# Square tiles on the four quarters of the array for the Gram matrices and low-rank projections of a recurrent branch

## The chip, the cores and the metric

The kernel runs on one core of a Trainium2 chip. The metric is the device time of one execution in microseconds. The engines are named as in the profile: PE is TensorE's matmul, PEld its weight loads, DVE is VectorE, ACT ScalarE, POOL GpSimd, SP the queue that issues the DMAs. L12 is line 12 of the kernel's file.

## The reference

One inference step through two layers of a hybrid backbone with 384 tokens (128 of context, 256 latents) of 1024 features. Each layer is a feed-forward half step, a token mixer and a second feed-forward half step. The mixer has three parallel branches: a windowed attention, a neighbourhood attention, and an RWKV-7 recurrence, one scan for each direction. Only the recurrence is touched here. Cut to what matters:

```python
for d, (wlo, alo) in enumerate(((wlo_f, alo_f), (wlo_b, alo_b))):      # two directions
    logw = -jax.nn.softplus(-(lp['decay_w0'][d] + jnp.tanh(wlo) @ lp['decay_up'][d])) - 0.5
    decay = jnp.exp(-jnp.exp(logw))
    a = jax.nn.sigmoid(lp['iclr_a0'][d] + alo @ lp['iclr_up'][d])
    k_d = k * (1.0 + (a - 1.0) * lp['k_a'])
    y_d, s_d = rwkv_scan(r32, decay, k_d, v32, kk, a, s0[:, d], reverse=(d == 1))

def step(S, inp):                                                       # of the scan
    r_t, w_t, k_t, v_t, kk_t, a_t = inp
    sa = jnp.einsum('bhvk,bhk->bhv', S, -kk_t)
    S = S * w_t[:, :, None, :] + sa[..., None] * (kk_t * a_t)[:, :, None, :] + v_t[..., None] * k_t[:, :, None, :]
    return S, jnp.einsum('bhvk,bhk->bhv', S, r_t)
```

`decay_up` and `iclr_up` are the low-rank projections, of rank 64, to 512 features. There are 8 heads of 64 features.

## The kernel before, in words

A layer goes through a feed-forward part, the two attentions, the recurrence, the mixer's output and a second feed-forward part. In the recurrence the eight heads go in four pairs p. A pair passes three stages: `rwkv_prepare` (the factors of the recurrence, with the low-rank projections), `rwkv_chunks` (each chunk of 64 tokens as a linear map of the state, with the Gram matrices) and `rwkv_scan`. In `rwkv_gen` the chunks of pair p are traced step by step among the scan of pair p - 1 and the preparation of pair p + 1.

Both directions d and both heads e of a pair lie on the two halves of the partitions: `half(e)` is the slice of 64 partitions that begins at 64 e. A matmul whose operands lie on 64 partitions uses 64 rows of the array. The operands of the stage are full float32, and each matmul of the source then makes two weight loads and two matmuls in the trace.

- The low-rank projections (L1425, L1426 and L1434, L1435; tile `up`): for each direction one matmul with 64 rows and all 128 columns of the array, over 384 tokens. `pws` and `pas` are two banks of PSUM each, taken from the tag `rw`, which has two banks in all (`rwp`). ACT reads a whole bank afterwards (tiles `th` and `ta`).
- The Gram matrices (L1499 to L1507; tile `pg`): for each direction, two groups, of four and of two chunks. For each chunk and head one matmul with 64 rows and 128 columns, over 128 columns of `arc`. Head e has its own bank `pg[e]`, from the tag `at`, which has three banks (`atp`). DVE then reads each bank once, masks it and writes `gt`.

Two other products of the stage matter for what follows, and are not touched. The tile `pm` is made of matmuls with 64 rows and 64 columns over 128 columns each, which go round the four quarters of the array in the order (0, 0), (1, 1), (0, 1), (1, 0) of row half and column half; it too takes two banks of the tag `at` for four chunks and then for two. The tile `p` (name `p3` in the code) has the same size of matmul on the two quarters of the diagonal.

The order on each engine is made when the kernel is built. A planner takes the instructions by priority, which is their place in the trace, moved ahead by `tc.high_priority(offset)`, and by its own estimate of when each is ready; a bank of PSUM is handed out to a tile as it comes free. An engine then runs its instructions in that fixed order. `tc.issue_after(x)` puts instructions behind x on its engine.

Dense products (the gates and the other branches' projections, `mixer_fill`) are woven into the recurrence: each small product calls `beside`, which adds a cost to a debt, and as long as the debt is over zero, takes the next step of dense products, of two chunks of 128 features with three matmuls each:

```python
    def beside(k, m, n):
        dense[1] += rate[0] * max(n / 600 / (4 if m <= 32 else 2 if m + k <= P else 1), 0.055)
        while dense[1] > 0 and dense[0] is not None:
            with tc.issue_after(rw_last[0].ins):
                b = next(dense[0], None)
            ...
            dense[1] -= b

    def rmm(out, lhs, rhs, **k):
        rw_last[0] = T.matmul(out, lhs, rhs, **k)
        beside(lhs.shape[0], int(np.prod(lhs.shape[1:])), int(np.prod(rhs.shape[1:])))
```

Here k is the number of rows of the array, m the number of columns, n the columns that stream. The functions:

Of the kernel before, what the change touches and what calls it, by code (L numbers as in the profile page):

```python
# [15 lines left out]
P = 128  # L16
# [51 lines left out]
A1 = 14  # L68
C_FIRST = ["tw", "al", "k0", "r0", "v0", "k1", "r1", "v1"]
# [122 lines left out]
# sets of four groups of 256 modulations; the first two are what the first chunks of features need, then the others  # L192
# [3 lines left out]
def _layout(inp):  # L196
    """Rearranges the inputs (permutations and concatenations only)."""
# [36 lines left out]
    # [l][d][h = (p, e)][v][k] -> [l][(e, k)][p][d][v]  # L234
# [8 lines left out]
def _weights(inp, order):  # L243
    """The large weights as 128 x 128 blocks in the order of their use."""
    f = {k: np.asarray(inp[k]) for k in {o[0] for o in order}}
    arows = np.concatenate([_a_q_cols(m) for m in range(4)])
    n = len(order)
    assert n == WS_UNITS * UNIT
    ws = np.empty((WS_UNITS, P, UNIT, P), next(iter(f.values())).dtype)
    for i, (name, l, k, c) in enumerate(order):  # L250
        rows = arows[P * k : P * k + P] if name == "proj_a" else np.arange(P * k, P * k + P)
        cols = _a_q_cols(c[1]) if isinstance(c, tuple) else slice(c, c + P)
        ws[i // UNIT, :, i % UNIT] = f[name][l, rows][:, cols]
    return ws.reshape(WS_SHAPE)
# [12 lines left out]
def _unlayout(r):  # L267
# [7 lines left out]
    st = r["o_st"].reshape(DEPTH, 2, HD, 4, 2, HD)  # l, e, k, p, d, v  # L275
# [4 lines left out]
class Engine:  # L280
    """An engine that knows its last instruction."""
# [14 lines left out]
def trunk(tc, I, O, order, taps=None, stop=None):  # L296
# [5 lines left out]
    def then(*engines):  # L302
        """Behind the last instruction so far of these engines."""
# [37 lines left out]
    class Stream:  # L341
# [16 lines left out]
        def ahead(self):  # L358
            """Out of the steady state: the unit after the next is split as soon as the last is used up."""
# [22 lines left out]
    def mm3(out, chunks, xs, after=()):  # L382
        """out += sum of W_k^T x_k, with both factors as sums of two float32r parts."""
# [7 lines left out]
    def mm3_steps(out, chunks, xs, step=2):  # L391
        """mm3 in steps of a few chunks, with what each costs."""
# [10 lines left out]
    def split(dst_h, dst_l, src, lo_eng):  # L403
        """src (SBUF or PSUM, float32) = dst_h + dst_l."""
# [30 lines left out]
    def ada_beside(pool, n):  # L435
        """The next n steps with the products on the vector engine: where that has time, and the tensor engine has not."""
# [38 lines left out]
    def ada_flush():  # L475
        """To columns: out[feature, (block, group, stream)]."""
# [20 lines left out]
    ax = [act.tile([P, NTOK], F32, name=f"ax{c}") for c in range(KD)]  # L497
    # (four more columns: see Norm)
# [8 lines left out]
    class Norm:  # L507
        """Layer norm over the features of y = alpha x + gate * out, chunk by chunk as out comes.
        The next phase's input is h = rs g1 (y - mu) + b1, g1 and b1 per feature and stream, rs and mu per token. Its
        first products W^T h run on z = g1 y, before rs and mu are known: rs W^T z - rs mu W^T g1 + W^T b1, with g1 and  # L510
        b1 as four more columns of z."""
# [34 lines left out]
        def add(self, c, po):  # L546
# [4 lines left out]
            if c == 0:  # L551
                # the table of Sqrt is there when it is needed
# [27 lines left out]
        def pilot(self):  # L580
            # about the mean of the first four chunks
# [14 lines left out]
        def products(self, chunks, xs, c):  # L596
            """The products of chunk c of out."""
# [14 lines left out]
        def finish(self, head=iter(())):  # L612
            """head: products of the next phase, in steps, from those on z to the last before h is needed."""
# [47 lines left out]
        def h(self, pool, c):  # L661
            """The next phase's input, in two parts."""
# [11 lines left out]
        def x(self):  # L674
            """alpha times the norm's output."""
# [5 lines left out]
    class Head:  # L681
        """The first products of a phase, on z: two groups of them, each chunk by chunk."""
# [25 lines left out]
        def begin(self, pool, norm, job, at):  # L708
            """The start of the phase: h follows the second group's products chunk by chunk; the first group's results."""
# [37 lines left out]
        def scaled(self, key, out, scale=1.0):  # L747
            """out = rs W^T z - rs mu W^T g1; returns scale W^T b1, a column per stream."""
# [21 lines left out]
    def gated(i, l, name, pool, xs, head, after):  # L770
        """128 features of silu(a) g, in two parts."""
# [70 lines left out]
    axd = es.enter_context(tc.tile_pool(name="axd", bufs=1, space=bass.MemoryType.DRAM))  # L842

    def mixer(l, nxt, next_head, head):
        spill = axd.tile([P, KD, NTOK], F32, name=f"axd{l}")
        gcd = axd.tile([P, KD, NTOK], F32, name=f"gcd{l}")
        with ExitStack() as st:
# [9 lines left out]
            with tc.tile_pool(name=f"rw{l}", bufs=1) as pool:  # L857
# [3 lines left out]
                def add(cost, until=None):  # L861
                    """Queues dense work behind the scans' last instruction."""
# [31 lines left out]
    def gate(l, i, m, th, head=None):  # L894
        """tanh(z / 2): the sigmoid is (1 + tanh(z / 2)) / 2."""
# [12 lines left out]
    def project(l, name, m, th, os):  # L908
        """2 merged += 2 gate * (o @ proj); the gate of branch A is in place."""
# [11 lines left out]
    def front_fill(l, keep, pool, w, oa, need, head):  # L921
        """The dense products beside the attention: what its next pair needs, then others."""
# [21 lines left out]
    def mixer_fill(l, keep, pool, w, ob, gcd):  # L944
        """Projections without a place in a chain: they keep the tensor engine busy beside the scans."""
# [12 lines left out]
    def softmax(pool, views, nk, sinks):  # L958
        """views: score tiles [P, nk] in PSUM; sinks: [P, n or 1] or None."""
# [22 lines left out]
    def transposed(pe, nk, pts):  # L982
        """pts: P^T destinations [P, nk // P, P]."""
# [6 lines left out]
    def token_major(pool, src, tag):  # L990
        """[128 features, 384 tokens] -> [token, block, feature]."""
# [10 lines left out]
    def key_stack(pool, src, e, bufs):  # L1002
        """Keys of one head, src[64 e :, :384], as [hi; hi] and [lo; lo] over the 128 partitions."""
# [9 lines left out]
    def query_stack(pool, src, e):  # L1013
        """Latent queries of one head, src[64 e :, :256], as [hi; lo] (in either order)."""
# [6 lines left out]
    def heads_pair(pool, q_ctx, q_lat, k_ctx, kst, vt, v_cache, bias, sinks, keep, name, done, backward=False):  # L1021
        """Two heads (on partitions 0..63 and 64..127) of both streams -> o^T split in two parts."""
        # context queries: full attention over the context
# [9 lines left out]
        # latent queries: latent keys, then the cached context keys  # L1033
# [44 lines left out]
    def rope(pool, src, dst):  # L1078
        """Rotates the latent columns of src [128, 384] into dst [128, 256]."""
# [9 lines left out]
    def attention(l, pool, keep, w, oa, ob, head, spill):  # L1089
        """Branches A and B, pair of heads by pair of heads, among steps of the dense products."""  # L1090
# [37 lines left out]
        for m in range(9):  # L1128
# [3 lines left out]
            # two pairs at a time: the first part of one before the end of the other  # L1132
# [31 lines left out]
    def branch_a(l, pool, ready, soon, head):  # L1164
        """Windowed grouped-query attention; pair m has the query heads m and m + 4."""
# [39 lines left out]
    def branch_b(l, pool, ready, soon):  # L1205
        """Neighbourhood attention; latent queries in reverse order: the bias is then a forward walk through na_rpb."""
# [45 lines left out]
    C_INDEX = {n: i for i, n in enumerate(["tw", "al", "gl"] + [f"{x}{i}" for x in "krv" for i in range(4)])}  # L1252

    def conv_gen(l, keep, pool, w, names):
        """Projections of the scans' inputs with the short convolution over time."""
        wsh = vcol(l, "w_shift")
        late = []
        for nm in names:
# [17 lines left out]
            elif nm[0] == "k":  # L1276
                # 1 / max(|k k_k|, 1e-12) per token and head
# [25 lines left out]
    def head_sums(out, sq):  # L1303
        """out[token, (block, head)] = sums of sq [128 features of two heads, 384] over each head."""
# [3 lines left out]
    def head_spread(pool, rn):  # L1308
        """[token, (block, head)] -> the same for each feature of the head, [128 features, 384], in PSUM."""
# [15 lines left out]
    def beside(k, m, n):  # L1325
        """Dense work beside a product: the tensor engine slows down where it has too little."""
# [464 lines left out]
```

## Time and profile before

| what | before |
|---|---|
| median of 3 runs | 2443.14 us (2442.91 to 2443.93) |
| span of the profiled execution | 2439.6 us |
| PE busy | 2297.4 us, 94% |
| DVE, ACT, POOL busy | 1696.6, 1056.4, 550.0 us |
| mean granted clock of TensorE | 0.983 of 2.4 GHz |

The span is the time from the first to the last instruction of the profiled execution. The profile gives no other time for that execution: what lies around its span is seen only as the 3.5 us between the span and the median of the timed runs. Busy time of PE is the union of the matmuls' spans, and matmuls overlap one another, so a busy PE does not always stream at its peak. The recurrence lies at 577 to 860 us in the first layer and at 1781 to 2065 us in the second.

### The profile page before, as it was taken

Reading aid. Unit: us, or ns where it says so; the run is one execution under the profiler, and the core shown is the slowest. Engines: PE = TensorE matmul, PEld = TensorE weight load, DVE = VectorE, ACT = ScalarE, POOL = GpSimd, SP = SyncE. Lnnn points to the kernel's source line nnn. Section 1 sums busy time; section 2 is a strip of 40 time slices with the busy share of each in tenths; the row PEclk is TensorE's granted clock in tenths of the full one; section 3 lists DMA queues with packets and bytes.
Section 4 is the critical chain, followed back from the end, with each engine's and each line's share of the span. In section 5 each row is a group of like instructions: output and inputs, shape, how many; then the busy total and the mean of one; then the engine's idle time right before and its main releaser. Section 6 shows DMA issues by size and latency. Waiting matters only on the chain.

```text
span 2439.6 us, 42863 instructions
## 1 busy us (share of the span) xinstructions
PE 2297.4 (94%) x17066; PEld 2106.5 (86%) x17066; DVE 1696.6 (70%) x2865; ACT 1056.4 (43%) x1942; POOL 550.0 (23%) x522
## 2 busy tenths in 40 slices
PE   7999999998899998999999999899989999999998
PEld 5999988897777788999889999889877777889997
DVE  3797886777767568786978954776787674665534
ACT  3333245655545445333243332555555454443332
POOL 2111422101122044211432113310022220542113
PEclk9999999999999999999999999999999999999999
DMA  8575644242111262665546743523321113534332
GB/s 314 193 240 198 191 122 130 84 111 78 40 57 47 72 209 95 191 217 180 180 147 205 244 130 122 154 81 91 112 70 39 51 50 90 204 102 140 130 121 87
DMA packets 125079, 324.54 MB, mean 133 GB/s; under 512 B 31568, under 2 KB 50256, under 8 KB 124880
## 3 DMA queue, kind: packets, MB, share of 16 engines
q1 hardware_dynamic: 124880, 321.81, 41.1%
q8 instruction: 134, 2.20, 0.4%
q14 instruction: 65, 0.53, 0.1%
HBM read 312.06 MB, written 9.70 MB: 132 GB/s over the span
## 4 chain that ended last, share of the span: by engine, by line
PE 71%; DVE 15%; ACT 5%; issue 4%; DMA 3%; POOL 2%; SPq 0%; POOLq 0%; ACTq 0%; DVEq 0%
PE po L399 5%; PE po L398 5%; PE po L397 5%; PE pa L387 4%; PE pg L389 4%; PE pa L388 4%; PE pg L387 4%; PE pg L388 4%; PE pa L389 4%; DVE lo L290 3%; DVE acc L290 2%; PE pz L397 2%; DMA adaw<-wada 2%; ACT hi L290 2%; PE pz L398 2%
## 5 line engine op out<-in xcount | busy, mean ns | idle before, releaser
L290 DVE TENSOR_TENSOR lo<-raw,hi 128x1024 fp32r<-128x1024 f32 (+1 forms) x472 | 583.8, 1246 | 305.9 <-ACT hi L290 303.8
L290 ACT ACTIVATE hi<-raw 128x1024 fp32r<-128x1024 f32 x418 | 441.7, 1058 | 785.0 <-issue 267.5
L290 DVE SCALAR_TENSOR_TENSOR acc<-adaw,cs,acc 128x1024 f32<-128x1024 f32 x224 | 292.3, 1327 | 0.0
L290 POOL TENSOR_TENSOR ul<-si,uh 128x384 fp32r<-128x384 f32 x88 | 126.3, 1435 | 579.3 <-ACT uh L290 579.3
L399 PE MATMUL po<-uh,lo 128*128 128x384 f32 x704 | 238.6, 339 | 6.3 <-DVE lo L290 6.3
L397 PE MATMUL po<-uh,hi 128*128 128x384 f32 x704 | 239.7, 340 | 0.0
L398 PE MATMUL po<-ul,hi 128*128 128x384 f32 x704 | 238.0, 338 | 0.0
L387 PE MATMUL pg<-zh,hi 128*128 128x384 f32 x656 | 224.1, 342 | 9.1 <-DVE si L290 9.1
L388 PE MATMUL pg<-zl,hi 128*128 128x384 f32 x656 | 223.8, 341 | 0.0
L389 PE MATMUL pg<-zh,lo 128*128 128x384 f32 x656 | 223.2, 340 | 0.0
L387 PE MATMUL pa<-zh,hi 128*128 128x384 f32 x632 | 216.2, 342 | 4.9 <-ACT si L290 4.4
L389 PE MATMUL pa<-zh,lo 128*128 128x384 f32 x632 | 213.8, 338 | 0.6 <-DVE lo L290 0.6
L388 PE MATMUL pa<-zl,hi 128*128 128x384 f32 x632 | 214.2, 339 | 0.0
L399 PEld LDWEIGHTS po<-uh,lo 128*128 128x128 f32 x704 | 133.5, 190 | 7.3 <-DVE lo L290 7.3
L397 PE MATMUL pz<-zh,hi 128*128 128x384 f32 x352 | 128.1, 364 | 8.5 <-ACT hi L290 5.7
L397 PEld LDWEIGHTS po<-uh,hi 128*128 128x128 f32 x704 | 133.7, 190 | 2.2 <-issue 0.8
L398 PEld LDWEIGHTS po<-ul,hi 128*128 128x128 f32 x704 | 133.5, 190 | 1.4 <-issue 0.8
L387 PEld LDWEIGHTS pg<-zh,hi 128*128 128x128 f32 x656 | 125.0, 191 | 10.0 <-ACT hi L290 6.7
L399 PE MATMUL pz<-zh,lo 128*128 128x384 f32 x352 | 126.3, 359 | 4.1 <-DVE lo L290 4.0
L387 PEld LDWEIGHTS pa<-zh,hi 128*128 128x128 f32 x632 | 119.1, 188 | 9.8 <-ACT si L290 5.3
L389 PEld LDWEIGHTS pg<-zh,lo 128*128 128x128 f32 x656 | 125.6, 191 | 1.6 <-issue 1.6
L388 PEld LDWEIGHTS pg<-zl,hi 128*128 128x128 f32 x656 | 125.0, 191 | 1.6 <-issue 1.6
(390 smaller groups left out, 5157.4 us busy)
## 6 DMA issues: line engine op xcount, KB each, us to landing
raw<-ws SPq DMA_DIRECT2D x418, 512.0 KB, 3.5
adaw<-wada SPq DMA_DIRECT2D x144, 512.0 KB, 4.8
bm<-rpb SPq DMA_DIRECT2D x64, 64.0 KB, 7.1
axd<-ax SPq DMA_DIRECT2D x16, 192.0 KB, 5.2
gcd<-gt SPq DMA_DIRECT2D x16, 192.0 KB, 4.7
gc<-gcd SPq DMA_DIRECT2D x16, 192.0 KB, 3.4
ax<-axd SPq DMA_DIRECT2D x16, 192.0 KB, 4.8
xt<-xt SPq DMA_DIRECT2D x8, 192.0 KB, 8.6
```

Of the source, the lines that this page charges most:

```text
L290: self.last = f(*a, **k)
L387: T.matmul(out, wh, xh, start=(k == 0), stop=False)
L388: T.matmul(out, wh, xl, start=False, stop=False)
L389: T.matmul(out, wl, xh, start=False, stop=(k == n - 1))
L397: T.matmul(out, wh, xh, start=(k == 0), stop=False)
L398: T.matmul(out, wh, xl, start=False, stop=False)
L399: T.matmul(out, wl, xh, start=False, stop=(k == n - 1))
```

## The change

A matmul of a Gram matrix or of a low-rank projection, with 64 rows and 128 columns of the array, becomes two with 64 rows and 64 columns, one for each half of the columns; all four of a chunk (Gram matrices) or of a pair of directions (projections) are issued in the order of `QUARTERS`. The banks, their readers and all other products stay as they are. Comments are left out of the diff.

```diff
+QUARTERS = ((0, 0), (1, 1), (0, 1), (1, 0))
...
     def rwkv_prepare(l, p, w, pool, x):
...
         pws = [rwp("up") for _ in range(2)]
-        for d in range(2):
-            rmm(pws[d][:, :NTOK], wl[half(d), 0, :], w["tw"][half(d), :], start=True, stop=True)
+        for d, m in QUARTERS:
+            rmm(pws[d][half(m), :NTOK], wl[half(d), 0, half(m)], w["tw"][half(d), :], start=True, stop=True)
...
         pas = [rwp("up") for _ in range(2)]
-        for d in range(2):
-            rmm(pas[d][:, :NTOK], wl[half(d), 1, :], w["al"][half(d), :], start=True, stop=True)
+        for d, m in QUARTERS:
+            rmm(pas[d][half(m), :NTOK], wl[half(d), 1, half(m)], w["al"][half(d), :], start=True, stop=True)
...
     def rwkv_chunks(l, p, w, pool, fix, x):
...
             for c0, n in ((0, 4), (4, 2)):
                 pg = [atp("pg"), atp("pg")]
                 for c in range(n):
-                    for e in range(2):
-                        rmm(pg[e][:, c * P : (c + 1) * P], bk[half(e), c0 + c].rearrange("p d t -> p (d t)"), arc[half(e), :, c0 + c, d, :], start=True, stop=True)
+                    for e, m in QUARTERS:
+                        rmm(pg[e][half(m), c * P : (c + 1) * P], bk[half(e), c0 + c, m, :], arc[half(e), :, c0 + c, d, :], start=True, stop=True)
```

## Rows read from the trace of the kernel before

**Rows 1.** The page: busy time of the engines; the chain that ended last, by engine.
```profile
PE 2297.4 (94%) x17066; PEld 2106.5 (86%) x17066; DVE 1696.6 (70%) x2865; ACT 1056.4 (43%) x1942; POOL 550.0 (23%) x522
...
PE 71%; DVE 15%; ACT 5%; issue 4%; DMA 3%; POOL 2%; SPq 0%; POOLq 0%; ACTq 0%; DVEq 0%
```
**Rows 2.** Windows of both recurrences: length, busy of PE, PEld, DVE, ACT, POOL, clock, DMA.
```profile
577.00:860.00 283.00, 260.94 (x3401) 214.85 (x3400) 199.88 (x416) 140.24 (x265) 59.94 (x87) 0.98 0.18 56
1781.00:2065.00 284.00, 262.70 (x3425) 216.06 (x3424) 201.98 (x423) 140.77 (x266) 60.48 (x87) 0.98 0.19 58
```
**Rows 3.** PE's groups by line, first recurrence: count, busy us, mean ns, idle before.
```profile
L1336 PE MATMUL pg<-arc,bk 64*128 64x128 f32 x192 | 20.3, 293 | 2.1 <-DVE gt L290 1.9
L1336 PE MATMUL p<-atq,xt 64*64 64x128 f32 x192 | 13.7, 273 | 0.0
L1336 PE MATMUL pm<-gt,atq 64*64 64x128 f32 x192 | 12.4, 282 | 1.5 <-DVE rp L290 1.1 <-ACT uv L290 0.4
...
L1336 PE MATMUL up<-al,wl 64*128 64x384 f32 x16 | 7.3, 535 | 0.0
L1336 PE MATMUL up<-tw,wl 64*128 64x384 f32 x16 | 7.3, 535 | 0.7 <-ACT th L290 0.7
```
**Rows 4.** Waits of DVE, first recurrence: who for whom, us in total, times, longest.
```profile
DVE mt L290 <- PE pm L1336: 15.5, 5, 8.2
DVE gt L290 <- PE pg L1336: 15.2, 10, 5.1
```
**Rows 5.** PE's timeline, Gram matrices: start, length, count, idle before.
```profile
595.10 1.60 PE L1336 MATMUL pg<-arc,bk 64*128 64x128 f32 x16
597.04 1.16 PE L1336 MATMUL pg<-arc,bk 64*128 64x128 f32 x8 [0.34 <-DVE gt L290]
...
725.92 1.38 PE L1336 MATMUL pg<-arc,bk 64*128 64x128 f32 x16
727.59 0.93 PE L1336 MATMUL pg<-arc,bk 64*128 64x128 f32 x8 [0.29 <-DVE gt L290]
```
**Rows 6.** Instructions of single tiles: count, shortest, median and longest ns.
```profile
L1336 PE MATMUL pg<-arc,bk x384: 271/272/374, 595.1 to 1995.0; 64*128 64x128 f32 x192
...
L1336 PE MATMUL pm<-gt,atq x384: 268/269/322, 639.9 to 2050.5; 64*64 64x128 f32 x192
...
L1336 PE MATMUL up<-tw,wl x32: 482/535/587, 577.6 to 1947.6; 64*128 64x384 f32 x32
```
**Rows 7.** PE's timeline, products already in quarters or on the diagonal.
```profile
639.92 0.93 PE L1336 MATMUL pm<-gt,atq 64*64 64x128 f32 x16
641.26 1.14 PE L1336 MATMUL pm<-gt,atq 64*64 64x128 f32 x24 [0.40 <-ACT uv L290]
...
643.84 0.65 PE L1336 MATMUL pm<-gt,atq 64*64 64x128 f32 x8 [0.61 <-DVE rp L290]
...
718.27 1.31 PE L1336 MATMUL pm<-gt,atq 64*64 64x128 f32 x30
719.84 0.87 PE L1336 MATMUL pm<-gt,atq 64*64 64x128 f32 x16 [0.27 <-DVE rp L290]
...
772.80 3.11 PE L1336 MATMUL p<-atq,xt 64*64 64x128 f32 x48
```
**Rows 8.** PE's timeline, the low-rank projections of two pairs.
```profile
669.46 0.91 PE L1336 MATMUL up<-tw,wl 64*128 64x384 f32 x2
...
673.10 0.91 PE L1336 MATMUL up<-tw,wl 64*128 64x384 f32 x2
...
743.07 0.91 PE L1336 MATMUL up<-tw,wl 64*128 64x384 f32 x2
743.91 0.44 PE L399 MATMUL pp<-o3h,lo 128*128 128x384 f32 x1
744.28 0.91 PE L1336 MATMUL up<-tw,wl 64*128 64x384 f32 x2
```
**Rows 9.** DVE's timeline, behind two batches of Gram matrices.
```profile
727.11 0.42 DVE L290 TENSOR_TENSOR gt<-pg,con 128x256 f32<-128x256 f32 x1 [3.98 <-PE pg L1336]
728.33 1.62 DVE L290 TENSOR_TENSOR gt<-pg,con 128x256 f32<-128x256 f32 x3 [0.80 <-PE pg L1336]
```
**Rows 10.** Windows around a stretch at half clock; columns as in rows 2.
```profile
755.00:757.00 2.00, 1.22 (x14) 0.79 (x14) 2.00 (x4) 1.35 (x4) 0.53 (x2) 1.00 0.03 8
757.30:760.60 3.30, 3.30 (x11) 3.30 (x12) 1.96 (x3) 0.54 (x2) 1.28 (x1) 0.51 0.39 109
```

## The prediction

> **What bounds the kernel now.** I read the page first: PE is busy 94% of the span, and the chain of work that ended last lies on PE for 71% of it [rows 1]. So a microsecond taken from PE's own stream counts, unless PE then waits for another engine. The change touches the recurrence only, so the windows of its two stretches came next [rows 2]: PE is busy in 523.6 of their 567 us (92%), DVE in 401.9. PE is the tightest engine here as well, with some 43 us in which it waits. The groups by line say what is at stake [rows 3]: in one layer the Gram matrices (`pg`) hold PE for 20.3 us in 192 instructions, the projections (`up`) for 14.6 us in 32. For both layers that is 70 us, or 2.9% of the kernel, and no gain can be larger. The waits show on which side the Gram matrices bind: DVE stands still for them 15.2 us in the first recurrence [rows 4], while PE waits for DVE's masking only 1.9 us [rows 3]. A shorter Gram batch would be felt at once.
>
> **How fast the halves run.** The timeline of the batches [rows 5] and the single durations [rows 6] belong together. A matmul over 384 columns takes 482 ns at the least, one over 128 columns 272 ns, so 256 columns more cost 210 ns, and 128 columns stream for 0.105 us. The batch of eight at 597.04 takes 1.16 us; without the 0.27 us of a single one that is 0.111 us each: one after another. The batch of sixteen at 725.92 takes 1.38 us, or 0.069 us each: partly two at a time. So the two row halves of the array already overlap in part. They can't do so always, since the two heads' banks come free at different times, and a batch of eight behind a wait for DVE is mostly one head.
>
> **The change: Gram matrices.** 192 instructions in a layer become 384, over the same 128 columns. What a round over four quarters costs is in the trace: `pm` has the same shape, the same order of quarters and the same banks [rows 7]. I price it three ways, each for 384 instructions of one layer against 20.3 us.
> - Fast end: from the batch of 8 (0.65 us) to the batch of 30 (1.31 us) each further matmul costs 0.03 us. If a direction's batches are 32 and 16, they take 1.37 + 0.89 = 2.26 us, and eight directions 18.1 us: 2.2 us less.
> - Middle: the five batches shown take 4.90 us for 94 matmuls, 0.052 us each, so 20.0 us: 0.3 us less.
> - Slow end: all of `pm` takes 12.4 us for 192 [rows 3], since some of it is chopped in pairs by dense work, so 24.8 us: 4.5 us more.
>
> The Gram batches are longer than those of `pm`, and none of those shown is chopped, so I take the point halfway between the fast end and the middle: 1.25 us less in a layer, 2.5 us in both, with ends of 4.4 us less and 9.0 us more. The gain isn't half of the 40.6 us, because the halves overlap already, and four quarters at 0.035 us each are three at a time, not four.
>
> **The change: projections.** Of 32 in the kernel, each takes 0.91 us as two instructions [rows 8]. The two of a pair stand apart: 3.64 us at 669, 1.21 us at 743. Both need a bank of the tag `rw`, which has two, and other tiles take them too. A quarter streams the same 384 columns; only its weight load is shorter. A matmul that starts cold shows it: 374 against 272 ns for a half, 322 against 269 ns for a quarter [rows 6], so about 0.05 us less. The planner can put (0, 1) in front of (1, 1), whose bank isn't free. I take it that the two quarters of a direction stay together and run at once: 32 x 0.05 = 1.6 us less. The ends: all four of a pair together hide one projection, about 0.86 us, in 16 pairs, 13.7 us less; all quarters apart add as much for each of 32, 27 us more. Neither is near the rows, since the bank keeps the directions apart and nothing keeps the two quarters of one bank apart.
>
> **What doesn't change.** The debt of dense work is the same: a half adds n / 600, a quarter half of that, twice. Banks, masks and DMAs stay; no DMA is issued or moved. There are 448 more matmuls with as many weight loads, in PE's queue alone; the rates taken from `pm` hold the issue of each, so I add nothing for it. If the offsets of priority, counted in instructions, now reach less far, a weight split may move behind its matmul; I have no row for that, and it is in the width.
>
> **The sum.** 2.5 + 1.6 = 4.1 us off PE. Of PE's time in the recurrence 92% is work and the rest waits, so I let 92% of it reach the end: 3.8 us. The profiled span of 2439.6 us becomes 2435.8 us, and with the 3.5 us between that span and the median, about 2439.3 us: 0.16% less. A change within 0.2% (4.9 us) can hardly be told from none here.
>
> **A page against the trace.** Behind the batches of 16 and 8, DVE masks for 0.42 and 1.62 us [rows 9], about 2.0 us in a direction, against 2.31 us of PE. The masking runs behind each batch, so a shorter batch moves it forward, and it is not yet the longer side. The Trainium skill's "TensorEngine Tiling (Array Packing)", section PSUM Bottleneck, says that packing speeds up the matmuls and not the emptying of PSUM. By it the gain of the Gram matrices would be nothing once the masks set the pace, and the sum would be 1.6 us.
>
> **Rivals.**
> - The quarters pay in full. First form: the Gram matrices reach the fast end, and PE loses 4.4 + 1.6 = 6.0 us, of which 5.5 us arrive: 2437.6 us. Second form: the projections of a pair go four at a time, too, 2.5 + 13.7 us, of which 14.9 us arrive: 2428 us. For it: `pm` holds 0.035 us a matmul over a batch of 30. Against the second form: the directions stand apart in all the rows shown.
> - Four quarters really run at once. A Gram matmul then costs 0.105 / 4 = 0.026 us, 384 of them 10.0 us, and both layers lose 20.6 us; with the 1.6 us, 20.4 us arrive: 2423 us. Against it: `pm` never comes below 0.035 us. The Trainium skill's same page, section Theoretical Speedup, states this case: up to twice for each side of a tile that is 64 or less.
> - The other side: the order of the quarters binds two banks. The output of direction 0 is whole only after (0, 1), which is traced behind (1, 1). If the planner doesn't put it ahead, PE stands at (1, 1) until the second bank is free, and ACT's `th` or `ta`, the dense work and the rest of PE's queue stand behind it. The price is at most the time that lies between the two projections now, 3.64 and 1.21 us, on the mean 2.4 us, in 16 pairs 39 us. It decides from 22% of that (8.7 us, the gain and 0.2%); at 30% the time is 2451 us. For it: the traced order. Against it: the planner fills waits with whatever is ready, as the dense work between the projections shows.
> - The quarters run only two at a time, as `p` does on the diagonal: 13.7 us for 192 [rows 3], so 27.4 us for 384, 7.1 us more in a layer, in both 14.2 us less the 1.6 us: 2455 us. `pm` speaks against it.
> - Nothing is gained: the masks, at 2.0 us in a direction nearly as long as PE's batches, or other waits behind them take it up. 2443 us, give or take 2.
> - The clock isn't one of them, but widens all: behind a stretch in which PE worked 1.22 of 2 us, the granted clock was 0.51 for 3.3 us, 1.2 GHz [rows 10]. One such stretch more or less is 1.7 us.
>
> **How the numbers follow.** The forecast 0.38 (all within 0.2%); the quarters in full 0.18 and 0.12, four at once 0.03 (faster); the banks 0.13 and two at a time 0.05 (slower); nothing gained 0.11 (same). Faster is 0.33, same 0.49, slower 0.18. The likeliest one's own range is 2436 to 2442 us: the sum with one stretch of slow clock either way and the two projections' terms in or out. The range for all reaches down to the second form of the gain, half of which lies below 2428 us (0.06, and 0.03 for four at once), and up to the banks at 30%, half of which lies above 2451 us (0.06), with two at a time (0.05) outside: 0.20 is left out.
>
> **What would show it.** In the profile after: `pg` with 768 instructions, 64 x 64, busy about 19 us in a layer, with batches of 32 of some 1.4 us; `up` with 128 instructions, in fours of about 0.86 us, and the two directions still apart. A batch of `pg` broken by dense work, or `up` in twos with other work between, would make the Gram or the projection term wrong, and PE's wait in front of `up` for ACT or DVE the order of the banks. If PE's busy time falls by 4 us and the span doesn't, the wait that grew names the step.

## The result and the profile after

The changed kernel takes 2479.59 us (median of 4 runs, 2474.05 to 2480.65) beside 2443.53 us before (4 runs): a ratio of 1.0153, interval [1.0133, 1.0172], some 36 us slower. The prediction was 2439.3 us in a range of 2428 to 2451.

The totals of the engines and of the chain (the page, sections 1 and 4) answer to [rows 1]:

```profile
PE 2330.7 (94%) x17514; PEld 2128.2 (86%) x17514; DVE 1696.0 (68%) x2865; ACT 1062.2 (43%) x1946; POOL 550.5 (22%) x522
...
PE 71%; DVE 15%; ACT 5%; issue 4%; DMA 2%; POOL 2%; SPq 0%; POOLq 0%; ACTq 0%; DVEq 0%
```

The windows of the two recurrences, from the first projection of a layer to the last product of its scan, first before, then after (columns as in [rows 2]):

```profile
577.60:861.20 283.60, 261.54 (x3408) 215.40 (x3409) 200.17 (x420) 139.64 (x264) 59.94 (x87) 0.98 0.18 57
1781.80:2063.10 281.30, 260.00 (x3410) 213.74 (x3409) 200.75 (x420) 139.76 (x264) 60.48 (x87) 0.98 0.19 58
```

```profile
581.70:880.90 299.20, 273.28 (x3632) 221.20 (x3633) 199.76 (x420) 142.62 (x266) 61.27 (x87) 0.94 0.18 54
1803.70:2103.00 299.30, 274.93 (x3634) 222.76 (x3633) 199.93 (x420) 142.46 (x266) 61.42 (x87) 0.94 0.17 54
```

Together they are 33.6 us longer: PE is busy 26.7 us longer and waits 6.9 us longer, so its share is as before (91 to 92%). What differs most is the last number but two, the granted clock: 0.94 instead of 0.98. The whole span and its mean clock say how much that is:

```profile
core 0: 2478.9 us, clock 0.969
```

A mean of 0.969 between full and half clock (2.4 and 1.2 GHz) means that 2 x 0.031 of the span, 154 us, ran at half clock; before, at 0.983 of 2439.6 us, 83 us did. Work that fills a microsecond at half clock would have taken half of it, so the 71 us more account for up to 35 of the 39 us between the two spans. (The clock has three digits, so such a difference is good to about 2 us.) That is an upper figure for this pair of executions. Of the 71 us, 17 lie ahead of the first projection, where both kernels issue the same instructions in the same order, so they are chance; 48 lie in the two recurrences, which is 24 of their 33.6 us. Over all four runs of the change (mean clock 0.9705) and 59 runs of before (0.9812) the account gives 27 of 38 us. So the clock has some seven tenths of the loss.

The products show it, and something else as well. These are PE's groups by line in the first recurrence, as in [rows 3]:

```profile
L1338 PE MATMUL pg<-arc,bk 64*64 64x128 f32 x384 | 21.2, 292 | 2.9 <-DVE gt L292 2.5
L1338 PE MATMUL pm<-gt,atq 64*64 64x128 f32 x192 | 14.7, 283 | 0.6 <-DVE rp L292 0.5
L1338 PE MATMUL p<-atq,xt 64*64 64x128 f32 x192 | 14.6, 303 | 0.0
L1338 PE MATMUL up<-tw,wl 64*64 64x384 f32 x32 | 9.2, 529 | 0.9 <-ACT th L292 0.7 <-DVE nkk L292 0.2
L1338 PE MATMUL up<-al,wl 64*64 64x384 f32 x32 | 7.0, 504 | 0.0
```

`pm` and `p`, which the change doesn't touch, take 14.7 and 14.6 us instead of 12.4 and 13.7. For `p` it is the clock: one of them takes 303 ns on the mean instead of 273. For `pm` it isn't: one takes 283 ns beside 282 before, and none of them runs at half clock; its 192 products stand in 24 pieces between other work instead of 16, so fewer of them overlap. So the new order costs PE something besides the clock.

The costliest place for the clock is in the first pair of heads of each layer. Windows there, before and after; the last line of each is the stretch at half clock in the second layer:

```profile
621.00:624.20 3.20, 1.44 (x99) 1.39 (x99) 3.20 (x7) 2.56 (x6) 0.00 (x0) 1.00 0.44 147
624.20:631.00 6.80, 6.25 (x117) 5.45 (x117) 3.10 (x8) 3.13 (x4) 0.00 (x0) 0.50 0.04 13
631.00:640.00 9.00, 9.00 (x161) 6.87 (x162) 4.39 (x9) 6.56 (x14) 0.31 (x2) 1.00 0.19 60
...
1829.10:1835.90 6.80, 6.56 (x143) 6.03 (x145) 2.51 (x8) 3.13 (x4) 0.00 (x0) 0.50 0.01 2
```

```profile
625.90:629.30 3.40, 1.86 (x101) 1.52 (x101) 3.21 (x6) 2.20 (x6) 0.00 (x0) 1.00 0.53 159
629.30:649.80 20.50, 18.55 (x259) 16.07 (x261) 6.35 (x17) 6.06 (x11) 0.00 (x0) 0.50 0.07 27
649.80:655.00 5.20, 5.20 (x62) 3.03 (x61) 0.76 (x4) 5.12 (x12) 0.00 (x0) 1.00 0.01 3
...
1851.30:1871.80 20.50, 19.41 (x266) 16.85 (x265) 6.55 (x17) 6.79 (x13) 0.00 (x0) 0.50 0.08 28
```

In both the clock falls behind a stretch in which PE, waiting for DVE, worked about half the time. Before, it was back after 6.8 us; after, it stayed at 0.50 for 20.5 us, with PE busy 18.55 of them. In both layers that is 27 of the 71 us. The timelines show what PE did, first in the stretch of before, then in the changed kernel's:

```profile
622.76 0.98 PE L1336 MATMUL pz<-yr,gt 16*32 16x16 f32 x96 [2.44 <-DVE yr L290]
...
627.97 0.67 PE L397 MATMUL pc<-zh,hi 128*128 128x384 f32 x1
...
630.31 0.67 PE L397 MATMUL pc<-zh,hi 128*128 128x384 f32 x1
```

```profile
627.30 0.98 PE L1338 MATMUL pz<-yr,gt 16*32 16x16 f32 x96 [3.35 <-DVE k L292]
...
631.98 0.94 PE L1338 MATMUL pz<-xt,gt 32*32 32x16 f32 x54 [1.85 <-issue]
...
639.07 0.67 PE L401 MATMUL pc<-zh,lo 128*128 128x384 f32 x1
...
641.13 0.52 PE L401 MATMUL pc<-zh,lo 128*128 128x384 f32 x1
...
643.86 1.54 PE L1338 MATMUL up<-tw,wl 64*64 64x384 f32 x2
645.20 5.28 PE L1338 MATMUL p<-atq,xt 64*64 64x128 f32 x48
```

In both, PE waits for DVE in front of the first small products (2.44 and 3.35 us), and dense work follows later. One of the new quarters stands in the changed kernel's stretch (two instructions), and it comes late, at 643.86. The rest is the triangular solve (`pz`), dense work (`pc`) and `p`, the same products as before, in another place of the stream. For the planner, the program that orders the instructions of each engine, had put much of the other work elsewhere from the first `up` on: of before's 5329 instructions of DVE, ACT and POOL together, 348 can't be matched in order with the changed kernel's. Up to there the order is the same on every engine. (ACT also loads its tables 44 times instead of 40, 1.28 us each. That isn't the loss: gram_quarters and halves_front60 below, with 40 and 36 loads, are 20 and 24 us slower than before.)

### The profile page after: what moved, and what is told of

The parts are those of the page before. It is cut to its first block, busy times and chain, and to the rows that moved or that the text cites. A ratio compares the mean times of both kernels' runs of the same rounds, so it can differ in the third digit from the quotient of the medians.

```text
span 2478.9 us, 43763 instructions
## 1 busy us (share of the span) xinstructions
PE 2330.7 (94%) x17514; PEld 2128.2 (86%) x17514; DVE 1696.0 (68%) x2865; ACT 1062.2 (43%) x1946; POOL 550.5 (22%) x522
## 4 chain that ended last, share of the span: by engine, by line
PE 71%; DVE 15%; ACT 5%; issue 4%; DMA 2%; POOL 2%; SPq 0%; POOLq 0%; ACTq 0%; DVEq 0%
PE po L401 5%; PE po L400 5%; PE po L399 5%; PE pa L389 4%; PE pg L391 4%; PE pg L389 4%; PE pg L390 4%; PE pa L390 4%; PE pa L391 4%; DVE lo L292 3%; PE pz L399 2%; ACT hi L292 2%; PE pz L401 2%; PE pz L400 2%; DVE acc L292 2%
```

## The experiments

Two theories. **A:** the quarter tiles themselves keep the granted clock low. **B:** the new order of all other work does. The table holds every kernel run; "span" and "clock" are of the profiled execution. "Clock's part" is (1 - clock) x span less the 41.5 us that this gives for before; "rest" is what of the difference in span it leaves. Both come from one execution of a kernel, and executions of one kernel differ: the profiled one of halves_front60 is 8 us slower than its three others. By the mean clock over all runs of a kernel, as above for the change, the clock's part is 28 of 44 us for quarters_priority_held, 18 of 29 for halves_front60, 30 of 33 for halves_in_after_order and 9 of 10 for quarters_in_old_order.

| kernel | us | ratio to before | span less 2439.6 | clock | clock's part | rest |
|---|---|---|---|---|---|---|
| the change | 2479.6 | 1.0153 [1.0133, 1.0172] | +39.3 | 0.969 | 35.3 | 4.0 |
| gram_quarters | 2458.1 | 1.0083 [1.0063, 1.0103] | +15.4 | 0.975 | 19.9 | -4.5 |
| proj_quarters | 2460.1 | 1.0091 [1.0068, 1.0114] | +16.3 | 0.976 | 17.4 | -1.1 |
| quarters_by_direction | 2476.6 | 1.0146 [1.0116, 1.0177] | +33.5 | 0.970 | 32.7 | 0.8 |
| quarters_priority_held | 2484.1 | 1.0184 [1.0156, 1.0212] | +43.9 | 0.970 | 33.0 | 10.9 |
| halves_front60 | 2467.2 | 1.0103 [1.0085, 1.0122] | +34.2 | 0.970 | 32.7 | 1.5 |
| halves_back220 | 2447.6 | 1.0027 [1.0012, 1.0042] | +11.1 | 0.976 | 17.3 | -6.2 |
| quarters_warm | 2490.7 | 1.0201 [1.0158, 1.0243] | +61.9 | 0.970 | 33.5 | 28.4 |
| halves_warm | 2477.7 | 1.0157 [1.0129, 1.0184] | +37.6 | 0.978 | 13.0 | 24.6 |
| gram_back120 | 2462.5 | 1.0090 [1.0068, 1.0111] | +17.6 | 0.975 | 19.9 | -2.3 |
| gram_front55 | 2455.6 | 1.0051 [1.0036, 1.0067] | +15.8 | 0.973 | 24.8 | -9.0 |
| gram_fill | 2481.9 | 1.0162 [1.0140, 1.0183] | +45.6 | 0.973 | 25.6 | 20.0 |
| quarters_fill | 2490.9 | 1.0196 [1.0181, 1.0211] | +49.4 | 0.963 | 50.6 | -1.2 |
| quarters_in_old_order | 2450.2 | 1.0046 [1.0030, 1.0062] | +15.6 | 0.975 | 19.9 | -4.3 |
| gram_in_old_order | 2444.6 | 1.0014 [0.9998, 1.0031] | -1.7 | 0.982 | 2.4 | -4.1 |
| proj_in_old_order | 2456.1 | 1.0055 [1.0034, 1.0075] | +18.5 | 0.974 | 22.4 | -3.9 |
| quarters_rows | 2464.8 | 1.0105 [1.0081, 1.0129] | +25.7 | 0.971 | 30.0 | -4.3 |
| halves_in_new_order | 2457.4 | 1.0068 [1.0042, 1.0094] | +17.1 | 0.973 | 24.8 | -7.7 |
| halves_in_after_order | 2471.3 | 1.0132 [1.0107, 1.0157] | +27.1 | 0.971 | 30.0 | -2.9 |

**One part alone (gram_quarters, proj_quarters).** One edit is undone, here the projections' (shown for one of its two places; the other kernel undoes the Gram matrices'):

```diff
-        for d, m in QUARTERS:
-            rmm(pws[d][half(m), :NTOK], wl[half(d), 0, half(m)], w["tw"][half(d), :], start=True, stop=True)
+        for d in range(2):
+            rmm(pws[d][:, :NTOK], wl[half(d), 0, :], w["tw"][half(d), :], start=True, stop=True)
```

> Only the Gram matrices in quarters, the projections in halves as before. Theory A (the quarters themselves keep the granted clock low: time goes with their number, 768 of 896 are here): 2470 to 2478 us. Theory B (the planner's changed order of the other work leaves a sparse stretch, and the clock falls there; what is in quarters does not matter): any value from 2435 to 2480 us, with the half-clock time of the profile explaining the difference to 2443.5 within 6 us (half of the extra time at half clock). The recorded rival of the two banks speaks of the projections alone: 2441 us.

> Only the projections in quarters, the Gram matrices in halves as before. Theory A: 2446 to 2450 us, since only 128 of 896 quarters are left. Theory B: any value from 2435 to 2480 us, again with the difference equal to half of the extra time at half clock within 6 us. The recorded rival of the two banks: nearly the whole loss is here, 2470 to 2480 us, with a wait of PE in front of `up`.

Each costs some 20 us, whether it brings 768 instructions in quarters or 128. Theory A, by the number of quarters, missed both: 2458 instead of 2470 to 2478, and 2460 instead of 2446 to 2450. The clock accounts for both differences within 5 us.

**Another order of the quarters (quarters_by_direction), and the planner's counter held (quarters_priority_held).**

```diff
-QUARTERS = ((0, 0), (1, 1), (0, 1), (1, 0))
+QUARTERS = ((0, 0), (0, 1), (1, 0), (1, 1))
```

```diff
-    def rmm(out, lhs, rhs, **k):
+    def rmm(out, lhs, rhs, back=0, **k):
         rw_last[0] = T.matmul(out, lhs, rhs, **k)
+        tc.cur_priority -= back
...
```

In the second, each call of the change passes `back=m`, 0 for the first half of the columns and 1 for the second.

> All in quarters, but traced in the order (0, 0), (0, 1), (1, 0), (1, 1), so that the two quarters of one bank stand together. The planned order of the other engines is nearly that of the changed kernel (12 of 2867 vector instructions moved). The recorded rival of the two banks: the loss goes, 2435 to 2448 us. Theories A and B: it stays, 2470 to 2485 us.

> All in quarters, but the second quarter of each half does not advance the counter of priorities, so that the planner's offsets reach as far as with halves; the planned order differs from both kernels. The products are those of the changed kernel. Theory A: 2474 to 2484 us. Theory B: the time moves with the order, by 10 us or more from 2479.6, and again the difference to 2443.5 equals half of the extra time at half clock within 6 us.

The first answers the recorded rival of the two banks: with the quarters of a bank together the loss stays, 2476.6 us, so that rival falls. (In the changed kernel's first recurrence PE waits 0.9 us in front of `up`, and 0.7 before.) The second moved the order, but not the time by the 10 us that theory B asked for, and 10.9 us of it is not the clock: a miss for that account. Its time is what theory A expected, to 0.1 us, so this run by itself speaks for A.

**Halves in another order (halves_front60, halves_back220).** No quarter is in these kernels; an offset of the planner is another.

```diff
-OA = 50
+OA = 60
```

```diff
-OB = 200
+OB = 220
```

> The kernel before, all in halves; only the planner's offset for the front work of the next pair is 60 instead of 50, which moves 344 of 2867 vector instructions to other places, more than the quarters do. The products are those of before. Theory A (quarters keep the clock low): no loss, 2434 to 2444 us. Theory B (a moved order does it, halves or quarters): slower, 2445 to 2480 us, with the difference equal to half of the extra time at half clock within 6 us.

> The kernel before, all in halves, with the planner's offset for the chunk work 220 instead of 200 (186 of 2867 vector instructions moved). Theory A: 2434 to 2444 us. Theory B: between 2440 and 2480 us, by the same account of the half-clock time; one of the two reordered kernels at least is over 10 us slower.

Both are slower. The first loses two thirds of what the quarters do, 24 us by the medians, at a clock of 0.970 in the profiled run and 0.975 to 0.976 in the others. Theory A can't say why.

**Products that fill the wait (quarters_warm, halves_warm).** Into the bank of the first small products, ahead of the transpose that they wait for, go two products that nothing reads (WARM is 2), and likewise one ahead of each of the next two transposes:

```diff
+                pz1 = atp("pz1")
+                for _ in range(WARM):
+                    T.matmul(pz1, C("ident"), ty.rearrange("p a b -> p (a b)"), start=True, stop=True)
                 V.transpose(yr.rearrange("p u (b c) -> p c b u", c=16), ty)
```

> The changed kernel with products added that nothing reads: two of 128 x 128 over 512 columns into the bank of the first small products, and two into that of the second, where TensorE waits for the vector engine's transposes. Theory A: the quarters still keep the clock low, 2474 to 2490 us. Theory B: the long stretch at half clock of the first pair (20.5 us in each layer) shrinks to 7 us or less, which gives back some 7 us in each layer; the added products cost at most 1 us a pair; 2460 to 2475 us.

> The kernel before with the same added products. Both theories: its stretches at half clock in the recurrence are short (6.8 and 3.4 us), so little is to be had, 2434 to 2446 us. With the kernel of quarters it shows whether the added products take away what the quarters seem to cost: theory B has the two within 15 us of each other, theory A 35 us or more apart.

In the kernel of quarters, windows of the first pair:

```profile
619.00:622.60 3.60, 0.16 (x1) 0.16 (x2) 3.30 (x6) 1.58 (x3) 0.00 (x0) 1.00 0.23 92
622.60:626.00 3.40, 3.40 (x5) 1.32 (x6) 2.96 (x6) 0.58 (x2) 0.00 (x0) 0.50 0.46 159
626.00:640.00 14.00, 14.00 (x366) 10.85 (x365) 6.24 (x15) 7.01 (x14) 0.00 (x0) 1.00 0.11 29
```

With full-width products in that place the clock is back after 3.4 us (6.8 in the second layer), not 20.5, though the quarters are all there. But the time rose: the added products keep PE busy some 20 us a layer, not 4 (in the groups of the first recurrence, 11.1 and 8.5 us), and other stretches at half clock came up later, 17.1 us from 704.5 and 20.5 us from 1936.7 on. The place is confirmed, the price of 2460 to 2475 us missed. The halves with the same products, expected at 2434 to 2446 us, took 2477.7 us: the price was missed there too. The two kernels are 13 us apart, as theory B asked (within 15) and theory A didn't (35 or more).

**Nearer orders and more dense work (gram_back120, gram_front55, gram_fill, quarters_fill).** `OC = 120` instead of 100, `OA = 55` instead of 50, and for the last two:

```diff
-RATES = (0.4, 0.2, 0.8, 0.3)
+RATES = (0.4, 0.4, 0.8, 0.3)
```

> Gram matrices in quarters, projections in halves, and the planner's offset for the scan of the pair before 120 instead of 100. That brings the order of the vector, scalar and GpSimd instructions nearer to that of before: 236 moved, against 376 with 100. The quarters are the same 768. Theory A (the quarters keep the clock low): no change from 2458, 2453 to 2465 us. Theory B (the order): the loss shrinks with the distance; the halves with 244 moved lost 6.6 us (a ratio of 1.0027) and the Gram quarters by themselves seem to give 4 us, so 2436 to 2450 us.

> Gram matrices in quarters, projections in halves, the planner's offset for the front work 55 instead of 50 (280 instructions moved against before, between the 236 and the 376 of the others). Theory A: 2453 to 2465 us. Theory B: 2438 to 2455 us, with the half-clock account within 6 us.

> Gram matrices in quarters, projections in halves, and twice as much dense work woven in beside the products of the second stage of a chunk (rate 0.4 instead of 0.2), just ahead of the small products in which the clock fell. Theory A: 2453 to 2465 us. Theory B: the long stretch at half clock of the first pair (20.5 us) is shorter, 2440 to 2455 us; if the dense work is then missing later, a stretch appears elsewhere and the time stays.

> The changed kernel, all in quarters, with the same doubled rate of dense work in the second stage of a chunk. Theory A: 2474 to 2484 us. Theory B: 2450 to 2472 us where the long stretches at half clock shrink; unchanged if they only move. Half-clock account within 6 us in either case.

Here theory B was too simple. Both nearer orders came out inside theory A's range and above theory B's. The count of moved instructions doesn't predict the time: 236 gave 2462 us, 280 gave 2456, 376 gave 2458. More dense work made both kernels slower; with all in quarters, the clock's part rose from 35 to 51 us, while with the Gram matrices alone 20 of the 45.6 us are not the clock's. Theory B's account by the clock, within 6 us, fails in seven of the table's nineteen lines, so an order can cost in other ways too.

**The two by two table (quarters_in_old_order, gram_in_old_order, quarters_rows, halves_in_new_order).** A list gives each instruction the place that it had in another kernel's plan as its priority, so that tiles and order can be changed separately. Only quarters_rows has no list: its plan is the planner's own, and the halves get it. In all kernels of quarters here and in the next pair the two quarters of a bank stand together, as in quarters_by_direction, and are charged for dense work as one half. The list:

```diff
+            self.tc.cur_priority = 10 * int(PLAN[Engine.count % len(PLAN)])
+            Engine.count += 1
             self.last = f(*a, **k)
...
```

> All in quarters, but every instruction gets as its priority the place that it has in the plan of the kernel before (the quarters that of their half), so that the order of all engines is that of before: 36 of some 6000 instructions off TensorE moved. Theory A (the quarters keep the granted clock low, in any order): 2465 to 2482 us, half-clock time 130 us or more. Theory B (the moved order does it): the time of before or a little less, 2436 to 2446 us, half-clock time 70 to 95 us.

> Gram matrices in quarters, projections in halves, in the order of the kernel before (4 instructions off TensorE moved). Theory A: 2455 to 2462 us, as with its own order. Theory B: 2434 to 2443 us: the order of before, less the 2 to 5 us by which the Gram matrices are shorter in quarters.

> All in quarters in the planner's own order, the two quarters of a half together and charged for dense work as one half. Its order differs from before in 778 places. It is the partner of the halves in its order. Theories A and B: slower than before, 2455 to 2495 us.

> All in halves, but with the places of the plan of that kernel of quarters as priorities: 128 instructions off TensorE moved against it, 370 against before. Theory A: no quarters, so the time of before, 2436 to 2446 us. Theory B: the order costs the halves as it costs the quarters, 2452 to 2495 us, and within 12 us of the kernel of quarters in that order.

Neither theory is right alone. In the old order the quarters lose 0.46%, 11 us, not 36, and not nothing; halves in an order of the quarters lose 0.68%, 17 us; the quarters in that order lose 1.05%, 25 us (2464.8 beside 2457.4 us for the halves, within the 12 us of theory B, though 128 instructions off PE still stand otherwise). So tiles and order each cost something here, and together about the sum. With the Gram matrices alone in quarters nothing can be told from no change (1.0014, and 1 lies in the interval), which shows also that the list by itself costs nothing that these runs can tell. What the Gram term does is best read there, in the same groups as [rows 3]:

```profile
L601 PE MATMUL pg<-arc,bk 64*64 64x128 f32 x384 | 19.3, 280 | 3.3 <-DVE gt L601 3.0
...
L601 PE MATMUL pm<-gt,atq 64*64 64x128 f32 x192 | 12.4, 282 | 1.5 <-DVE rp L601 1.1 <-ACT uv L601 0.4
```

`pm` takes its 12.4 us again, and `pg` 19.3 instead of 20.3 us. But PE now waits 3.0 us for DVE's masking in front of `pg`, instead of 1.9: by these rows the microsecond gained is spent there. DVE's own wait for `pg`, 15.2 us in [rows 4], hardly shrinks:

```profile
DVE gt L601 <- PE pg L601: 14.7, 10, 5.1
```

Its timeline beside [rows 5], in the first and in the third pair, shows where: PE waits 1.69 us instead of 0.34 in the first. In the third the wait is as before (0.31 and 0.29), and the two batches take 2.18 us instead of 2.31:

```profile
594.38 1.58 PE L601 MATMUL pg<-arc,bk 64*64 64x128 f32 x34
597.66 1.09 PE L601 MATMUL pg<-arc,bk 64*64 64x128 f32 x14 [1.69 <-DVE gt L601]
...
723.80 1.31 PE L601 MATMUL pg<-arc,bk 64*64 64x128 f32 x32
725.42 0.87 PE L601 MATMUL pg<-arc,bk 64*64 64x128 f32 x16 [0.31 <-DVE gt L601]
```

**The changed kernel's own order, and the projections (halves_in_after_order, proj_in_old_order).** The same list, with the changed kernel's plan on halves, and with the plan of before on projections in quarters.

> All in halves, with the places of the changed kernel's own plan as priorities: 76 instructions off TensorE stand otherwise than in the changed kernel, 328 otherwise than before. Theory A (the quarters): the time of before plus little, 2438 to 2450 us. Theory B (the order): most of the changed kernel's loss, 2462 to 2480 us. From the runs in the old order (quarters by themselves 11 us slower, with 18 us more at half clock) I expect both to have a part: 2460 to 2472 us.

> Only the projections in quarters, in the order of the kernel before (36 instructions off TensorE moved). If the parts add, it is what is left between the two kernels in that order, 5 to 8 us slower than before (2445 to 2449 us); if the projections cost nothing by themselves and the Gram matrices' 5 us are all, 2438 to 2443 us.

Without one quarter, the order of the changed kernel costs 1.32%, against 1.53% with them. Its windows in the first pair, the second layer's stretch at half clock, and both recurrences:

```profile
622.30:625.70 3.40, 0.37 (x43) 0.38 (x45) 3.16 (x6) 2.63 (x6) 0.00 (x0) 1.00 0.14 37
625.70:646.20 20.50, 20.50 (x337) 17.37 (x327) 8.98 (x20) 9.07 (x16) 0.31 (x2) 0.50 0.13 47
646.20:650.00 3.80, 3.80 (x58) 2.77 (x54) 0.00 (x0) 3.73 (x11) 0.00 (x0) 1.00 0.00 0
...
1837.40:1851.10 13.70, 12.77 (x267) 11.25 (x267) 8.59 (x20) 6.41 (x12) 0.00 (x0) 0.50 0.25 79
...
577.70:874.20 296.50, 275.86 (x3408) 226.92 (x3409) 201.50 (x420) 142.39 (x266) 59.59 (x87) 0.93 0.17 55
1793.50:2091.10 297.60, 277.29 (x3410) 228.38 (x3409) 200.83 (x420) 142.40 (x266) 58.52 (x87) 0.93 0.17 55
```

The stretch of 20.5 us at half clock is there, behind the same wait, with halves; in the second layer it is 13.7 us. This is the plainest view of what the order does: the same products as before, 3408 and 3410 of them, keep PE busy 31.6 us longer in the two recurrences, at a clock of 0.93 instead of 0.98, while PE waits no longer than before.

The projections by themselves cost 0.55% in the old order, more than the 0.2 to 0.3% expected. Whether the parts add can't be told: 0.14 and 0.55% against 0.46% for all quarters is within the intervals. Their own time is no reason: in the first recurrence the two groups of `up` are 7.3 and 7.0 us, 0.3 us less than in [rows 3]; the clock's part is 22 us.

## Why the prediction was wrong

- **The step that failed** is "What doesn't change", with the last rival, "The clock isn't one of them, but widens all". I took the order of all other work as given, and the clock as one stretch of 1.7 us either way. The changed kernel has 71 us more at half clock, up to 35 us in time and some seven tenths of the loss, and its order alone brings 1.32% with halves. That another order might cost something stood in the text only as a weight split that moves; a rival by the name of "the planner puts the other work elsewhere" was missing. The one case that reached as high as the measured time was the two banks at nearly their full price (39 us); that it comes near is chance, for that rival fell.
- **The Gram term:** 1.25 us less in a layer was the forecast. In the old order it is 1.0 us with the Gram matrices alone in quarters, so the size was nearly right. That 92% of it arrive was not: PE waits 1.1 us more for DVE, and DVE's wait for `pg`, from which I had read that "a shorter Gram batch would be felt at once", shrank by 0.5 us only. This is the rival "nothing is gained". The rule of the Trainium skill's "TensorEngine Tiling (Array Packing)", section PSUM Bottleneck, that the emptying of PSUM isn't sped up, agrees with this trace (a mask takes 550 ns at the median with halves and with quarters, and PE's wait for the masks grew from 1.9 to 3.0 us), and I gave it too little.
- **The projection term:** 0.8 us in a layer was the forecast, and 0.3 us is measured in the old order. Where the four quarters of a pair stood together (at 690.98 us in the changed kernel's timeline) they took 0.88 us for both directions, as the rival's second form had it; the one at 643.86 us above stands alone.
- **The other rivals:** the two banks fell (quarters_by_direction, 2476.6 us). Four at once and two at a time are excluded by `pg` at 19.3 us for 384, 0.050 us each; four at once asked for 0.026 and two at a time for 0.071.
- **By order and by tiles:** the order alone costs 1.32% [1.07, 1.57], most of the 1.53% [1.33, 1.72], measured with halves in nearly that order (76 instructions off PE stand otherwise). In the old order, the tiles' own part is 0.46% [0.30, 0.62]; the two sum to a little more than the whole, within the intervals. Both come mostly through the clock: in that old order the mean clock over the runs is 0.9775 (10 runs) beside 0.9812 for before (59 runs), (0.0225 x 2448) - (0.0188 x 2439) = 9 us of the 11. With the changed kernel's order it is up to 27 of 38 us; the pieces of `pm` and 6.9 us more of waiting stand beside it.
- **What stays open:** why the clock comes back after 6.8 us in one order and after 20.5 in the other. In the old one, seven dense products stand almost alone from 627.97 us on, and the clock is back at 631.0; but in the changed kernel seven stand in a row from 639.07 to 641.13 us, and it isn't. So what PE works on in the last microseconds doesn't decide alone. With full-width products in the wait the clock was back after 3.4 us (quarters_warm); what decides between the two orders is not shown. Nor does the order fix the length: in halves_in_after_order the two layers issue the same instructions in the same order on PE, DVE, ACT and POOL for over 100 us from their first projection on, and the stretch lasted 20.5 us in the one and 13.7 in the other. (Each kernel has one profile only.) Why the quarters in the old order lose 9 us to the clock isn't settled: their stretch in the first pair is 10.2 us, between the two, but 36 instructions off PE still stand otherwise there.

```profile
624.50:634.70 10.20, 8.98 (x228) 7.86 (x230) 4.49 (x11) 4.20 (x7) 0.00 (x0) 0.50 0.15 50
```

No version that beats the kernel before was found.

## What to carry to other kernels

Where a planner orders the instructions, an edit to one product is an edit to all the work behind it: price the new order as a term of its own, or hold the old one (each instruction's old place as its priority) and look at the tiles alone. Before a gain of some microseconds is put into a sum, compare the time that half clock can cost in both traces (one minus the mean clock, times the span, an upper figure); here it was some seven tenths of the result. A product that gets faster in front of an engine that empties its banks only moves the wait.

## What was not expected of the hardware

- TensorE stayed at 1.2 GHz while it was busy without a gap: 20.50 of 20.50 us at a granted clock of 0.50 (halves_in_after_order), on dense products, small ones of 32 x 32 and `p` of 64 x 64 in turn. The Trainium skill's "TensorE: Matmul & The Clock Gate", section "What's actually happening", ties the clock to how busy the engine has been; busy time, as the profile counts it, was not enough here.
- The same instructions in the same order, up to the first projection, took 577.6 us in the profile of before, 10 of them at half clock, and 581.7 us in that of the changed kernel, 27 of them at half clock. And the runs of before beside these experiments, 59 in all, go from 2433.6 to 2448.6 us, the faster ones at the higher mean clock (0.985 at 2435.3, 0.977 at 2444.5). So some 10 us of any single comparison here can be the clock's own. Half of the time at half clock is too high a price there: the two runs at 0.985 and the five at 0.977 lie 12 us apart on the mean, and (1 - clock) x span gives 20.
